# A transformer block on one NeuronCore: order of the row sums, the rotary steps and the head turns, order of the PSUM banks, and fixed places for the first stage's weights

## The chip, the core and the metric

The kernel runs on one core of a Trainium2 chip. The core has five engines that work through their own queues in order and meet at semaphores: TensorE (matmuls and transposes, called PE in the profile, its weight loads PEld), VectorE (DVE), ScalarE (ACT), GpSimd (POOL) and SyncE (SP, which issues most DMAs). Matmul results land in PSUM, eight banks of 128 x 512 float32; everything else lies in SBUF, and large data in HBM.

The metric is the device time of one execution in microseconds. Before the change three runs took 2041.41, 2048.91 and 2049.46 us, median 2048.91.

## The reference, cut to what matters

One encoder layer on 512 tokens of width 2048, everything in float32:

```python
h = rmsnorm(x, g_mix)
qa, ka, va, qb, kb, vb = split(h @ w_in)          # 1024, 256, 256, 1024, 1024, 1024 columns
q, k = axial_rope(rmsnorm(qa, g_q)) * hd**-0.5, axial_rope(rmsnorm(ka, g_k))   # mixer A: 8 heads, 2 kv heads
A = softmax(q @ k.T) @ va
q, k = partial_rope(qb) * hd**-0.5, partial_rope(kb)                            # mixer B: 8 heads
B = softmax(q @ k.T + log_multiplicity_mask) @ vb       # three dilated windows merged by their denominators
x = x + concat(rmsnorm(A, g_out_a), rmsnorm(B, g_out_b)) @ w_out
h2 = rmsnorm(x, g_ffn)
x = x + (silu(h2 @ w_gate) * (h2 @ w_up)) @ w_down
out = rmsnorm(x, g_final)
```

## The kernel before, in words

**Precision.** A float32 product is made of three matmuls. Each operand is split into a high part (ScalarE copies it in a rounded format) and a low part (VectorE subtracts), and `mm3` (line 200) multiplies high by high, high by low, low by high.

**Units.** The weights stream through a list of units in a fixed order, and the order is written out by hand: the main loop (lines 1190 to 1220) goes through the list, and at each unit it emits loads up to 20 or 24 us ahead, splits up to 8 or 10 us ahead (`prepare`, line 1163), then the unit's own matmuls, then what is hooked to that unit, then *side tasks*. Each unit gives a credit (1.0, in the attention 1.42 and later 1.9), and a side task is emitted when the credit covers its cost. So the program's order, and with it the order on each engine's queue, comes from these numbers. A plain unit is 12 matmuls of 512 columns, a block's unit 6.

**The input projection.** The first chunk makes k, v of mixer A (`kvA`, 16 plain units). While it runs, `x_prep` (line 266) transposes x on TensorE and splits it, and `row_squares` (line 317) sums the squares of whole rows on ScalarE, from which `make_r1` gets the row scale that each result is multiplied by when it leaves PSUM. Then come two blocks (`in_block`, line 752): two groups of 512 columns at a time, with seven products of half-size operands in place of eight. Each block's products are named m1 to m7, 8 units each, and accumulate in three pairs of banks, z, y and x. The first block makes vB, the second qA. Four plain chunks follow for qB and kB. All results are written to HBM and read back (`reload`, line 410) when the attention wants them.

**The attention** is made of side tasks beside the four plain chunks and the first half of the output projection. `norm_rope` (line 356) does the norm and the rotary steps of mixer A for one group of 128 tokens in two tasks, `rope_partial` (line 443) those of mixer B. A head takes four slots; in a slot (`task`, line 553) TensorE transposes a block of the probabilities of a head six slots earlier (`pt`), multiplies one of seven slots earlier with v (`pv`), makes one score block (`score`), and three and two slots ahead of a head its q and k are transposed (`tq`, `tk`).

**Memory.** `bank` (line 94) takes PSUM banks from one pool of eight, `Raw.load` (line 215) weight buffers from pools with a count each (`RAWS`), `slot` (line 83) SBUF pieces of 128 x 512; which free piece is taken is left to the framework.

**Behind it** lie the output projection, eleven gate/up blocks and the down projection, in the same form of block.

Of the kernel before, what the change touches and what calls it, by code (L numbers as in the profile page):

```python
# [19 lines left out]
P = 128  # L20
# [30 lines left out]
RAWS = {"raw": 6, "craw": 24, "craw40": 20, "draw6": 20, "draw8": 28}  # L51
W_TILES = {"wi": 12, "wo": 12}
# [5 lines left out]
TURN_LAG = 6  # L58
COLUMN_BLOCKS = 2
# [7 lines left out]
def encoder_block(ctx, tc, x, g_mix, w_in, g_q_a, g_k_a, g_out_a, g_out_b, w_out, g_ffn,  # L67
# [26 lines left out]
    def bank(base):  # L94
        return pp.tile([P, 512], F32, tag="b", bufs=8, name=nm(base))
# [8 lines left out]
    xs = [None] * KD  # L104

    def load_x(k):
        xs[k] = slot(f"x{k}", F32, (P, NT, P))
        nc.sync.dma_start(xs[k], x[0, :, k * P:(k + 1) * P].rearrange("(t p) c -> p t c", p=P))
# [28 lines left out]
    warm_ps = bank("warm")  # L137
# [5 lines left out]
    def load_gain(dst, rows, eng):  # L143
        raw = slot("gain")[:KD, :P]
        lo = 0
        for src, n in rows:
            eng.dma_start(raw[lo:lo + n], src[0].rearrange("(k p) -> k p", p=P))
            lo += n

        def finish():  # L150
            ps = bank("gain")
            nc.tensor.transpose(ps[:, :KD], raw, ident[:KD, :KD])
            nc.scalar.activation(dst, ps[:, :KD], AF.Copy)
        return finish
# [6 lines left out]
    def load_consts():  # L161
        for i, g in enumerate((g_q_a, g_k_a)):
            nc.sync.dma_start(gqk[:, i, :], row_bcast(g, HD))
        for i in range(2):
            ctab.append(slot("ctab", F32, (P, NT, HD)))
            nc.sync.dma_start(ctab[i], c_axial[:, i])
        nc.sync.dma_start(ropeb, c_partial)
        nc.sync.dma_start(mask, c_mask)
# [40 lines left out]
    units = []  # L209

    class Raw:
# [3 lines left out]
        def load(self):  # L215
            if self.t is None:
                self.t = wp.tile([P, self.width], F32, tag=self.tag, bufs=RAWS[self.tag], name=nm("raw"))
                for src, dst in self.pieces(self.t):
                    if self.first:
                        for a in range(src.shape[1]):  # L220
                            nc.sync.dma_start(dst[:, a], src[:, a])
                            load_x(self.first + a)
                    else:
                        nc.sync.dma_start(dst, src)

    class Unit:
# [10 lines left out]
        def split_hi(self):  # L237
            src = self.raw.t[:, self.sub * 512:(self.sub + 1) * 512]
            self.src, self.w = src, (wslot(self.tag), wslot(self.tag))
# [19 lines left out]
    xpair = [None] * (KD // 2)  # L259
# [6 lines left out]
    def x_prep(k):  # L266
        ps = bank("xt")
        for t in range(NT):
            nc.tensor.transpose(ps[:, t * P:(t + 1) * P], xs[k][:, t, :], ident)
        i, half = divmod(k, 2)  # L270
        if half == 0:
            xpair[i] = sp.tile([P, 4 * 512], F32, tag="xpair", bufs=3, name=nm("xpair"))
# [9 lines left out]
        else:  # L282
            nc.scalar.activation(flat, ps, AF.Copy, scale=gain)
            nc.scalar.activation(hi, view, AF.Copy)  # L284
            nc.vector.tensor_tensor(lo, view, f32(hi), op=OP.subtract)
        if half == 0:
# [23 lines left out]
    ss1 = small()  # L310
    rows = {}

    def load_rows(t):
        rows[t] = sp.tile([P, D], F32, tag="rows", bufs=2, name=nm("rows"))
        nc.sync.dma_start(rows[t], x[0, t * P:(t + 1) * P, :])

    def row_squares(t):
        nc.scalar.activation(rows[t], rows[t], AF.Square, accum_out=ss1[:, t:t + 1])

    def col_sums(src):  # L320
        ps = bank("cs")
        for t in range(NT):
            nc.tensor.matmul(ps[:, t:t + 1], src[:, t * P:(t + 1) * P], ones, start=True, stop=True)
        return ps[:, :NT]
# [3 lines left out]
    def make_r1():  # L328
        r1["r"] = rsqrt_mean(ss1, NT, D)
# [3 lines left out]
    tabs = {}  # L333

# [65 lines left out]
    def post_plain(name, ps):  # L400
        for t in range(NT):
            e = slot("ev" + name)
# [3 lines left out]
            else:  # L406
                nc.scalar.activation(e, ps[t], AF.Copy, scale=r1["r"][:, t:t + 1])
            store(name, t, e, nc.scalar)

    def reload(name, dst):  # L410
        assert stored[name] == NT, name
        for t in range(NT):
            dst[t] = slot(name)
            nc.sync.dma_start(dst[t], spill[name][t])

    def split_vA(t):
# [4 lines left out]
        src = kA[t][:, 256:]  # L421
        nc.scalar.activation(h, src, AF.Copy)
        nc.vector.tensor_tensor(l, src, f32(h), op=OP.subtract)

    def transpose_k_a(kv):
        ps = bank("kt")
        for t in range(NT):
            nc.tensor.transpose(ps[:, t * P:(t + 1) * P], kA[t][:, 256 + kv * HD:256 + (kv + 1) * HD], ident)
        kTA[kv] = split(ps, "kT", at=((2, 4 + 2 * kv), (2, 5 + 2 * kv)))

# [30 lines left out]
    class Head:  # L461
# [5 lines left out]
        def tq(self):  # L467
            ps = bank("qt")
# [6 lines left out]
            self.q = split(ps, "qT")  # L475

        def tk(self):
# [3 lines left out]
            ps = bank("kt")  # L481
# [3 lines left out]
            self.k = split(ps, "kT")  # L485

        def score(self, t):
            if t == 0:
                self.negm, self.z, self.rz = small(), small(), small()
            ps = bank("sc")  # L490
# [6 lines left out]
            else:  # L497
# [3 lines left out]
                nc.scalar.activation(p, p, AF.Exp, bias=nmx, scale=-1.0, accum_out=z)  # L501
            nc.vector.reciprocal(rz, z)
# [3 lines left out]
        def pt(self, kb):  # L506
            ps = bank("pt")
            for t in range(NT):
                nc.tensor.transpose(ps[:, t * P:(t + 1) * P], self.p[t][:, kb * P:(kb + 1) * P], ident)
            self.pT = split(ps, "pT")  # L510
            self.pTs = getattr(self, "pTs", {})
            self.pTs[kb] = self.pT

        def pv(self, kb):
            if kb == 0:
                self.o = bank("o")
# [7 lines left out]
        def fin(self):  # L524
# [8 lines left out]
            else:  # L533
                sq = slot("sq")
                nc.scalar.activation(sq, self.o, AF.Square)
                nc.gpsimd.tensor_tensor(acc[self.kind], acc[self.kind], sq, op=OP.add)
            if self.h == 7:
# [7 lines left out]
    def head_tasks(spec):  # L545
        n = len(heads)
        heads.append(Head(*spec))

        def at(slot):
            h, i = divmod(slot, NT)  # L550
            return (heads[h], i) if 0 <= h < len(heads) else (None, i)

        def task(s):
            head, i = at(s - TURN_LAG)
            if head:
                head.pt(i)
            head, i = at(s - TURN_LAG - 1)
            if head:
                head.pv(i)
                if i == NT - 1:  # L560
                    head.fin()
            head, i = at(s)
            if head:
                head.score(i)
            head, i = at(s + 3)
            if head and i == 0:
                head.tq()
            if head and i == 1:
# [706 lines left out]
```

## Time and profile before

| | |
|---|---|
| median of the runs | 2048.91 us |
| profiled execution, its own time | 2048.41 us |
| its span, first to last instruction | 2046.6 us |
| mean granted TensorE clock | 0.990 |
| PE busy | 2002.8 us (98%) |
| DVE busy | 1560.9 us (76%) |
| ACT busy | 1110.0 us (54%) |

A row of the waits view reads: engine and result that waited, what ended the wait, us in total, how often, the longest. A row of a timeline reads: start, duration, engine, line, operation, result and operands, and in brackets the engine's idle time before it with what ended it. A group row gives count, busy us and mean ns, then the idle time before the group. A clock of 0.5 means that TensorE got half of its full clock.

### The profile page before, as it was taken

To read this page: it belongs to the slowest core of one execution; us is meant where nothing else is said; L and a number is where in the kernel's file an instruction comes from. 1 tells how busy PE (TensorE), PEld (TensorE's weight loads), DVE (VectorE), ACT (ScalarE), POOL (GpSimd) and SP (SyncE) were. 2 spreads that over 40 slices of the span, in tenths; PEclk is the share of its full clock that TensorE was granted. 3 is DMA by queue.
4 is the path that set the end of the run, shared out by engine and by line. 5 is a ranking of instruction groups with operands and counts; after the bars stand their busy time and mean duration, and the time that the engine had idled before them with its cause. 6 is when DMAs were issued, how large, how long until landed. Compare 5 with 4: busy or idle time off the path is not lost.

```text
span 2046.6 us, 27457 instructions
## 1 busy us (share of the span) xinstructions
PE 2002.8 (98%) x9019; PEld 1639.0 (80%) x9019; DVE 1560.9 (76%) x2768; ACT 1110.0 (54%) x1952; POOL 126.4 (6%) x155
## 2 busy tenths in 40 slices
PE   9999999999999999999999999999999999999997
PEld 7788877887778888888888888888888888788886
DVE  5778756566764479778778788788788987977876
ACT  7655344455543466545555545545555666656655
POOL 0000101000000000000000000000000021111122
PEclk9999999999899999999999999999999999999999
DMA  8876532235234457458468367477477699778855
GB/s 273 299 249 203 174 103 93 89 117 176 98 97 151 158 180 240 136 197 293 138 217 290 119 239 262 132 254 250 133 252 233 201 282 249 188 172 268 216 115 179
DMA packets 232336, 394.82 MB, mean 193 GB/s; under 512 B 21712, under 2 KB 70656, under 8 KB 231552
## 3 DMA queue, kind: packets, MB, share of 16 engines
q1 hardware_dynamic: 205696, 330.33, 48.0%
q0 software_dynamic: 14800, 32.51, 7.9%
q10 hardware_dynamic: 11696, 30.23, 4.3%
q8 instruction: 70, 1.15, 0.2%
q14 instruction: 74, 0.61, 0.1%
HBM read 329.28 MB, written 63.70 MB: 192 GB/s over the span
## 4 chain that ended last, share of the span: by engine, by line
PE 86%; DVE 6%; issue 3%; ACT 2%; DMA 1%; POOL 1%; ACTq 0%; POOLq 0%; DVEq 0%; SPq 0%
PE zc L202 12%; PE zc L203 12%; PE zc L204 12%; PE yc L203 6%; PE yc L202 6%; PE yc L204 6%; PE xc L202 3%; PE xc L203 3%; PE xc L204 3%; PE pj L204 3%; PE pj L203 3%; PE pj L202 3%; PE pw L202 3%; PE pw L204 3%; PE pw L203 3%
## 5 line engine op out<-in xcount | busy, mean ns | idle before, releaser
L688 ACT ACTIVATE tw<-raw 128x512 fp32r<-128x512 f32 x1036 | 627.1, 628 | 496.1 <-DVE raw L725 321.7
L691 DVE TENSOR_TENSOR tw<-raw,tw 128x512 fp32r<-128x512 f32 x1036 | 693.3, 686 | 186.4 <-ACT tw L688 182.6
L202 PE MATMUL zc<-tw,arena 128*128 128x512 f32 x1184 | 465.6, 393 | 2.5 <-ACT ev L1045 1.7
L203 PE MATMUL zc<-tw,arena 128*128 128x512 f32 x1184 | 463.1, 391 | 4.5 <-DVE tw L691 4.4
L204 PE MATMUL zc<-tw,arena 128*128 128x512 f32 x1184 | 462.7, 391 | 0.0
L725 DVE TENSOR_TENSOR raw<-raw,raw 128x512 f32<-128x512 f32 x592 | 405.1, 684 | 1.4 <-DMA raw<-in_w_gate_up_dram 1.4
L203 PEld LDWEIGHTS zc<-tw,arena 128*128 128x128 f32 x1184 | 223.2, 189 | 52.9 <-DVE tw L691 7.8
L202 PEld LDWEIGHTS zc<-tw,arena 128*128 128x128 f32 x1184 | 223.2, 188 | 49.9 <-ACT ev L1045 2.4
L204 PEld LDWEIGHTS zc<-tw,arena 128*128 128x128 f32 x1184 | 222.9, 188 | 46.7
L202 PE MATMUL yc<-tw,arena 128*128 128x512 f32 x592 | 231.4, 391 | 0.0
L203 PE MATMUL yc<-tw,arena 128*128 128x512 f32 x592 | 230.6, 390 | 0.8 <-DVE tw L691 0.8
L204 PE MATMUL yc<-tw,arena 128*128 128x512 f32 x592 | 230.5, 389 | 0.0
L1046 POOL DMA_DIRECT2D x1d<-ev x76 | 66.4, 971 | 1154.4 <-ACT ev L1045 1142.3
L202 PE MATMUL pj<-w,arena 128*128 128x512 f32 x320 | 129.5, 405 | 3.4 <-ACT arena L284 1.9
L203 PEld LDWEIGHTS yc<-tw,arena 128*128 128x128 f32 x592 | 111.2, 188 | 24.3 <-DVE tw L691 1.7
L204 PEld LDWEIGHTS yc<-tw,arena 128*128 128x128 f32 x592 | 111.1, 188 | 23.2
L202 PEld LDWEIGHTS yc<-tw,arena 128*128 128x128 f32 x592 | 111.1, 188 | 22.8
L203 PE MATMUL pj<-w,arena 128*128 128x512 f32 x320 | 126.2, 395 | 2.2 <-DVE w L245 2.2
L204 PE MATMUL pj<-w,arena 128*128 128x512 f32 x320 | 126.6, 396 | 0.0
L202 PE MATMUL xc<-tw,arena 128*128 128x512 f32 x296 | 115.4, 390 | 0.0
L203 PE MATMUL xc<-tw,arena 128*128 128x512 f32 x296 | 115.3, 389 | 0.1
L204 PE MATMUL xc<-tw,arena 128*128 128x512 f32 x296 | 115.2, 389 | 0.0
(205 smaller groups left out, 2440.1 us busy)
## 6 DMA issues: line engine op xcount, KB each, us to landing
raw<-in_w_gate_up_dram SPq DMA_DIRECT2D x616, 256.0 KB, 5.3
raw<-in_w_in_dram SPq DMA_DIRECT2D x180, 256.0 KB, 4.5
raw<-in_w_down_dram SPq DMA_DIRECT2D x176, 256.0 KB, 7.0
forms<-pair SPq DMA_DIRECT2D x22, 896.0 KB, 5.3
x1d<-ev POOLq DMA_DIRECT2D x76, 256.0 KB, 6.8
fr<-forms ACTq DMA_DIRECT2D x35, 512.0 KB, 4.9
raw<-in_w_out_dram SPq DMA_DIRECT2D x32, 512.0 KB, 4.2
x<-in_x_dram SPq DMA_DIRECT2D x32, 256.0 KB, 4.9
```

The lines of the kernel that those rows point to most:

```text
L202: nc.tensor.matmul(dst, ah, bh, start=start, stop=False, skip_group_check=chained)
L203: nc.tensor.matmul(dst, ah, bl, start=False, stop=False, skip_group_check=chained)
L204: nc.tensor.matmul(dst, al, bh, start=False, stop=stop, skip_group_check=chained)
L688: nc.scalar.activation(self.pair[:, 0], self.src, AF.Copy)
L691: nc.vector.tensor_tensor(self.pair[:, 1], self.src, f32(self.pair[:, 0]), op=OP.subtract)
L725: nc.vector.tensor_tensor(t[dst], t[src[0]], t[src[1]], op=OP.add if form == "m6" else OP.subtract)
L1046: nc.gpsimd.dma_start(x1_dram[2 * cb + j, row], e, accum_op=OP.add)
```

## The change

- **Row sums in halves.** Each row of 2048 is loaded and squared in two halves, eight steps hooked to units 13 to 28 in place of four at units 11 to 14; the row scale is made at unit 29. kvA is therefore written without the scale, and k and v are scaled after their reload (`scale_k`, `split_vA`). The first block's first eviction comes 7 units later.
- **Order of the blocks.** qA first, vB second.
- **Early rotary steps and turns.** Tables and q steps come ahead of v and k. The second group of q steps is spread over slots 6 to 9. B's rotary steps come 8 and 7 slots ahead of their head pair, their reload 11 ahead; q is transposed 4 slots ahead, k 2. The value product comes 8 slots after the score.
- **PSUM banks in order of return.** Eight fixed banks in a queue: `bank()` takes the first, `release` puts a bank back at the end.
- **Fixed places.** Until the second block's end, x, the weights of the first chunk and of both blocks, and kvA's evictions use 20 fixed places of 128 x 512 (24 for a while), taken and returned in the same way; meanwhile only two double buffers of the next chunk's weights may be loaded. Split pairs, rows and results also get fixed tiles.
- **Others.** q, k reload as one transfer each; the constants load later, the mask at slot 20; buffer counts of later stages change (`RAWS`).

```diff
-RAWS = {"raw": 6, "craw": 24, "craw40": 20, "draw6": 20, "draw8": 28}
-W_TILES = {"wi": 12, "wo": 12}
+RAWS = {"raw": 6, "craw": 24, "craw0": 24, "kraw": 9, "craw40": 18, "draw6": 21, "draw8": 28}
+W_TILES = {"wi": 10, "wo": 12}
+VALUE_LAG = 8
-    def bank(base):
-        return pp.tile([P, 512], F32, tag="b", bufs=8, name=nm(base))
+    banks = deque(pp.tile([P, 512], F32, tag=f"b{n}", name=f"b{n}") for n in range(8))
+    def bank():
+        return banks.popleft()
+    def release(*tiles):
+        banks.extend(tiles)
+    stage = wp.tile([P, 20, 512], F32, tag="stage", bufs=1, name="stage")
+    homes = deque(stage[:, n] for n in range(20))
+                self.homed = bool(homes) and self.tag != "raw"
+                self.t = homes.popleft() if self.homed else wp.tile([P, self.width], F32, tag=self.tag,
+                                                                    bufs=RAWS[self.tag], name=nm("raw"))
-    def row_squares(t):
-        nc.scalar.activation(rows[t], rows[t], AF.Square, accum_out=ss1[:, t:t + 1])
+    def load_rows(n):
+        rows[n] = in_turn(rows_turn, 2, [P, D // 2], F32, "rows")
+        t, half = divmod(n, 2)
+        nc.sync.dma_start(rows[n], x[0, t * P:(t + 1) * P, half * (D // 2):(half + 1) * (D // 2)])
+    def row_squares(n):
+        nc.scalar.activation(rows[n], rows[n], AF.Square, accum_out=ss1[:, n:n + 1])
+    for n, at in enumerate((13, 15, 18, 20, 22, 24, 26, 28)):
+        hook(at - 3, lambda n=n: load_rows(n))
+        hook(at, lambda n=n: row_squares(n))
+    hook(29, make_r1)
+    hook(21, more_homes)
-            head, i = at(s - TURN_LAG - 1)
+        head, i = head_at(s - VALUE_LAG)
-            head, i = at(s + 3)
+        for lead in ("tq", "tk"):
+            head, i = head_at(s + {"tq": 4, "tk": 2}[lead])
...
+        todo = light(0.4, table_tasks()) + q_tasks(0)
+        todo += light(0.4, vs + kn)
+        todo += [heads[0].tq] + light(0.6, [lambda kv=kv: transpose_k_a(kv) for kv in range(NKV)])
+        todo += [heads[0].tk]
+        at(3, light(0.1, [lambda: reload("qA1", qA[1])]))
+        at(20, light(0.1, [lambda: nc.sync.dma_start(mask, c_mask)]))
+        for n, f in enumerate(q_tasks(1)):
+            at(6 + n // 2, [f])
+        for j in range(4):
+            s = NT * (NHA + 2 * j)
+            at(s - 11, light(0.1, [lambda j=j: reload(f"qkB{j}", qkB[j])]))
+            for n, f in enumerate(b_ropes(j)):
+                at(s - 8 + n, [f])
...
-    last.after("m5", 0, load_consts)
-    last.after("m5", 3, lambda: reload("kvA", kA))
+    last.after("m3", -2, load_consts)
+    last.after("m3", 0, leave_homes)
+    last.after("m5", 0, fewer_homes)
+    last.after("m3", 1, lambda: reload("qA0", qA[0]))
+    last.after("m3", 2, lambda: reload("kvA", kA))
...
+                    if homing[0] and len(homes) <= (2 if xs[KD - 1] is None else 4 if done["load"] < 24 else 0):
+                        return
+                    if homing[0] and raw.tag == "raw" and sum(r.tag == "raw" for r in live) >= 2:
+                        return
```

295 lines of the change are left out of this document (165 added, 130 removed).

## The prediction

> **What bounds the kernel now.** I began with the page's busy times and clock row, then cut the span into stretches to see where TensorE is not fed.
>
> ```profile
> span 2046.6 us, 27457 instructions
> PE 2002.8 (98%) x9019; PEld 1639.0 (80%) x9019; DVE 1560.9 (76%) x2768; ACT 1110.0 (54%) x1952; POOL 126.4 (6%) x155
> PEclk9999999999899999999999999999999999999999
> ```
>
> TensorE is busy 2002.8 of 2046.6 us. The change neither adds nor removes a matmul of 512 columns, so it can only win what TensorE loses to waits and to a reduced clock. The stretches show where that is; the columns are length, busy time (instructions) of PE, PEld, DVE, ACT and POOL, granted clock, DMA share, GB/s.
>
> ```profile
> 50.00:100.00 50.00, 45.21 (x187) 34.79 (x186) 38.28 (x70) 32.23 (x53) 2.75 (x4) 0.97 0.88 311
> 150.00:200.00 50.00, 50.00 (x222) 41.42 (x221) 41.33 (x68) 25.77 (x43) 1.64 (x3) 1.00 0.58 194
> 250.00:300.00 50.00, 44.86 (x199) 36.34 (x199) 31.00 (x74) 18.07 (x40) 2.23 (x2) 0.93 0.36 106
> 300.00:350.00 50.00, 45.62 (x207) 35.01 (x206) 34.04 (x94) 19.68 (x42) 4.45 (x4) 1.00 0.27 89
> 450.00:500.00 50.00, 47.95 (x236) 38.45 (x235) 32.69 (x79) 28.27 (x60) 3.58 (x3) 1.00 0.45 144
> 500.00:550.00 50.00, 43.94 (x207) 34.80 (x205) 38.13 (x95) 26.02 (x53) 2.60 (x2) 0.93 0.49 162
> 550.00:600.00 50.00, 45.41 (x212) 36.18 (x212) 35.67 (x86) 25.15 (x53) 3.88 (x3) 0.93 0.24 75
> 600.00:650.00 50.00, 49.69 (x214) 39.70 (x215) 18.95 (x30) 21.61 (x39) 3.99 (x3) 0.94 0.47 157
> ```
>
> The stretch 150:200 is the undisturbed one: 222 matmuls in 50 us, 0.225 us each. Idle time in the other seven is 4.8 + 5.1 + 4.4 + 2.1 + 6.1 + 4.6 + 0.3 = 27.4 us. A clock of 0.93 over 50 us is 3.5 us of lost work, so the clock adds 1.5 + 3.5 + 3.5 + 3.5 + 3.0 = 15 us. Together 42 us lie in the projection and the attention, which this change rewrites; the gate/up and down stages behind them it touches only in buffer counts.
>
> The waits say who is late.
>
> ```profile
> PE qt L474 <- DVE qkB L453: 5.7, 8, 1.7
> PE qt L474 <- DVE qA L383: 5.1, 2, 4.2
> PE pt L509 <- DVE pTl L194: 3.1, 4, 1.4
> PE pj L203 <- DVE w L245: 2.2, 3, 1.4
> PE kt L484 <- DVE qTl L194: 2.1, 3, 0.7
> PE pj L202 <- ACT evqkB L405: 1.5, 4, 0.6
> PE o L203 <- DVE pTl L194: 1.5, 2, 1.3
> ```
>
> No engine is full here (DVE 31 to 38 of 50 us): TensorE waits because in-order queues reach a piece of work late, or because a PSUM bank is taken that was read a moment ago (pt, kt and pj<-evqkB: a transpose or matmul waits for the *previous* tile's last read).
>
> **Term A, row sums in halves (50 to 100 us).** ScalarE there:
>
> ```profile
> 43.99 1.90 ACT L318 ACTIVATE rows<-rows 128x2048 f32<-128x2048 f32 x1
> 45.80 0.18 ACT L318 ACTIVATION_READ_ACCUMULATOR rows<-rows 128x1 f32 x1
> 46.59 0.63 ACT L284 ACTIVATE arena<-xpair 128x512 fp32r<-128x512 f32 x1
> 56.55 1.92 ACT L318 ACTIVATE rows<-rows 128x2048 f32<-128x2048 f32 x1 [0.46 <-DMA rows<-in_x_dram]
> 64.22 0.69 ACT L407 ACTIVATE evkvA<-pj,smalls 128x512 f32<-128x512 f32 x1 [1.82 <-POOL smalls L184]
> 49.66 0.33 SPq L315 DMA_DIRECT2D rows<-in_x_dram  x1
> ```
>
> Four squares of 1.90 + 0.18 us fall into 14 us, then the kvA evictions wait 1.8 us for the row scale. After the change eight halves are spread over units 13 to 28 of the stream, and kvA is stored unscaled, so nothing at unit 15 waits. A half, interpolated between the 0.63 us row and the 1.90 us row, is 1.04 + 0.18 = 1.2 us; eight are 9.8 us against 8.3, which is 1.5 us more ScalarE work, hidden because it is spread over 16 units. Added too are four scalings of 256 columns for k (0.5 us each) after the reload. Against it: a half's buffer comes back only four column units (4 x 6 x 0.225 = 5.4 us) before its next square, and 1.2 us of that is the square. The last whole row was issued at 49.7 and used at 56.6, 6.9 us, so a half may land up to 2.7 us late, in two chains of buffers; if the 8 us by which splits run ahead did not hide that, it costs 4 us. Between -4 and the whole 6.3 us I take 4, nearer the gain since the split lead lies between.
>
> **Term B, the turn from the blocks to attention (250 to 300 us).** DVE had a hole at the turn, and ScalarE shows why.
>
> ```profile
> 223.94 0.42 DVE L423 TENSOR_TENSOR arena<-kvA,arena 128x256 fp32r<-128x256 f32 x1 [5.12 <-ACT arena L422]
> 220.63 0.69 ACT L764 ACTIVATE evqA<-zc,smalls 128x512 f32<-128x512 f32 x1 [7.48 <-PE zc L204]
> 218.82 2.81 SPq L414 DMA_DIRECT2D qA<-qA  x4
> 242.60 0.28 DVE L366 CUSTOM_DVE_ANT_0 ra<-qA 128x128 f32<-128x128 f32 x1
> 246.42 0.69 DVE L383 TENSOR_TENSOR qA<-qA,smalls 128x512 f32<-128x512 f32 x1
> 260.11 0.69 DVE L383 TENSOR_TENSOR qA<-qA,smalls 128x512 f32<-128x512 f32 x1
> ```
>
> DVE stands 5.1 us for a V split that sits on ScalarE behind the block's last eviction, is then full from 223.9 to 260.8, and the first query transpose, which needs the last rotary step, waits for it. The change puts the tables and the query steps first, which need no ScalarE; the block order makes qA old enough to be read. The hole can go. But what is late next is the load: qA's reload is now one transfer of 1 MB, behind some three weight pairs of 512 KB on SP's queue, since these were held to two while the fixed stage lived; and the two key transposes move to the end of the list, with only one query transpose between them and the last k step. DVE's work from 223.9 to 260.8 is 36.9 us, some 4 of them around the key transposes, so 33; begun at 218.8 it ends at 252. TensorE comes to that point at 260.8 - 5.1 = 255.7. The lead is 4 us, and a longer hole while qA lands brings the wait back. Whole gain: 5.1 + 3.5 clock = 8.6. If 2.6 MB at 194 GB/s (the stretch 150:200) keep qA until some 13 us after 218.8, the wait is 4 us longer than now: -4. I take 4, between the ends, nearer the gain since the weights were prefetched in part.
>
> **Term C, second group of query steps (300 to 350 us).** One token's query steps take DVE 4.5 us (242.60 to 247.1). Eight tasks of cost 0.8 stood in a row; at 1.42 per unit of 12 matmuls (2.7 us) two of them give TensorE 3.1 us. So DVE fell behind by over 1 us per token, and its weight splits with it (pj<-w). Now a score slot of cost 1.5 stands between each pair: 2.9 us of projection and six matmuls more, while DVE has the following to do for a slot.
>
> ```profile
> L194 DVE TENSOR_TENSOR pTl<-pt,pTh 128x512 fp32r<-128x512 f32 x64 | 44.0, 688 | 48.5 <-ACT pTh L193 47.9 <-issue 0.5
> L503 DVE TENSOR_SCALAR p<-p,smalls 128x512 f32<-128x512 f32 x64 | 34.0, 531 | 2.2
> L495 DVE TENSOR_REDUCE smalls<-sc 128x1 f32<-128x512 f32 x32 | 22.0, 689 | 7.7 <-PE sc L204 6.3
> L502 DVE RECIPROCAL smalls<-smalls 128x1 f32<-128x1 f32 x64 | 10.5, 164 | 59.2 <-ACT p L496 30.5 <-ACT p L501 28.7
> ```
>
> That is 2.1 us and a weight split, 2.8, against 4.3 or more on TensorE. The backlog shrinks in the slot, and I take 3.4 of the 4.4 us (bounds 0 and 4.4).
>
> **Term D, the heads (450 to 620 us).** These are the first query transposes of a B head pair after its rotary steps:
>
> ```profile
> 509.62 0.33 PE L474 MATMUL qt<-fixed,qkB 128*128 128x128 f32 x1 [1.66 <-DVE qkB L453]
> 510.54 0.37 PE L474 MATMUL qt<-fixed,qkB 128*128 128x128 f32 x1 [0.59 <-DVE qkB L453]
> 511.46 0.47 PE L474 MATMUL qt<-fixed,qkB 128*128 128x128 f32 x1 [0.56 <-DVE qkB L453]
> 512.39 0.48 PE L474 MATMUL qt<-fixed,qkB 128*128 128x128 f32 x1 [0.45 <-DVE qkB L453]
> 514.25 1.12 PE L509 MATMUL pt<-fixed,p 128*128 128x128 f32 x4 [1.39 <-DVE pTl L194]
> ```
>
> The steps stood one task ahead of the transposes; now they stand three slots ahead, over 10 us, with the same instructions. Of the 5.7 us of qt<-qkB I expect all. Banks handed out in order of return mean that a taker gets the one longest idle: kt<-qTl 2.1 and pt<-pTl 3.1 go (half of them lie in 450 to 620). The value product is two slots behind its transpose instead of one: o<-pTl, 1.5 us, mostly goes. I take 9.5 of the 13.1 us idle here. Of the three reduced clocks (10 us) I take two, 7: each stands in a stretch with such waits. Bounds: 3 (banks only) to 23.
>
> Here a rule speaks against me. The Trainium skill, TensorE: Matmul & The Clock Gate, Why this matters for your kernels, asks only for "No PE-idle gaps >~3µs between matmul bursts" to keep the clock. By it the three late reductions, where no wait is over 1.7 us, would have another cause and stay, and the time would be 7 us higher, 2024. The trace disagrees with it: 0.93 stands beside waits of 1.7, 0.6, 0.6, 0.5 and 1.4 us in a row.
>
> **Term E, the rest.** A wait's end costs a little that busy time hides (single transposes above of 0.33 to 0.48 us): some 30 waits less by 0.1 us, 3 us. The buffer counts of the last gate/up block (20 to 18) and the first down blocks (20 to 21) bind where a load is late; I take 0, bounds -3 and +1 (a wait like those of 0.6 to 1.9 us above, once or twice). First-chunk splits in eight pairs instead of six, two copies of 4 columns and the mask's later load lie beside other work: 0, or -1 where uncovered.
>
> Sum: 4 + 4 + 3.4 + 16.5 + 3 = 31 us. The profiled execution took 2048.4 us, 1.8 around its span and 0.5 below the median of the runs shown, 2048.9. So 2017; terms moving together within half their bounds make 2009 to 2026.
>
> **The rivals.**
> *Only the heads gain* (0.15). A and B come to nothing, because ScalarE waits for halves and the turn waits for qA's load. For: 50 to 100 us moves 311 GB/s at a DMA share of 0.88. Against: the split lead. Then C, D and 2 of E, 22 us, less the 4 that one of them may cost: 2030.
> *All of it goes* (0.12): 42 + 4, 2002. For: no engine is full; against: B's thin lead.
> *The order only changes who is last* (0.12). The chain score, DVE, ScalarE, DVE, transpose, ScalarE, DVE limits the heads, and TensorE waits at pt instead of qt. For: ScalarE ends 47.9 us of DVE's gaps. Against: those gaps cost TensorE nothing for most heads. Then D gives 3, the others half: about 9, so 2040, within 0.5%.
> *Room in SBUF decides* (0.11), and it is slower. The stage of 20 places, q and k reloaded as whole 1 MB tiles, and one more pair of transposed probabilities per head all lie in one memory. If a head's slots must wait for the value product two slots behind, every score slot waits. SP already waits for such room:
>
> ```profile
> SPq L436 <- DVE pTl L194: 23.3, 3, 15.7
> ```
>
> It decides once ScalarE's p or pT waits for a release instead of for data; one 0.6 us wait (as pj<-evqkB) in each of 64 + 9 slots is 44 us, so 2048 - 31 + 44 = 2061. Against: the stage ends before attention.
>
> **How the numbers follow.** Forecast 0.50. About 0.5% (10 us) is what a measurement of this kernel can tell from none, that is 2038.7 to 2059.2. Faster is 0.50 + 0.15 + 0.12 = 0.77, same 0.12, slower 0.11. The range 2003 to 2045 leaves out slower and a little of the full gain.
>
> **What would show it.** A: no square of 2048 columns, no zc<-tw wait before 80 us, clock 1.00 there. B: no 5 us hole in DVE at the turn, and qt<-qA gone; wrong if kt (its keys) waits instead. C: pj<-w under 1 us. D: qt<-qkB, kt<-qTl, pt<-pTl gone, clock 1.00 from 500 to 620. Wrong altogether if ScalarE's or DVE's waits inside the slots are ended by older slots' reads.

## The result, and the profile after

The changed kernel takes 2024.82 us (2023.18 to 2026.50), the kernel before 2048.16 us over all its runs beside it: a ratio of 0.9893, with a 95% interval of 0.9869 to 0.9916. That is a gain of 23.3 us, where 31 were predicted. The profiled execution took 2025.08 us. These are the page's span and busy times of the changed kernel:

```profile
span 2023.3 us, 27380 instructions
PE 1989.5 (98%) x9019; PEld 1632.9 (81%) x9019; DVE 1558.8 (77%) x2771; ACT 1112.5 (55%) x1964; POOL 125.9 (6%) x155
```

The same 9019 matmuls and transposes are busy for 13.3 us less, and the span outside them is shorter by 10.0 us (33.8 in place of 43.8). So over half of the gain is in *shorter* busy time, and nearly all of that is the granted clock: its mean rose from 0.990 of the 2046.6 us to 0.996 of the 2023.3, some 12 us of lost clock less. Only the rest of the gain is idle time that a view of waits would list.

The stretches of the changed kernel, with the columns of the prediction (length, busy time of PE, PEld, DVE, ACT, POOL, granted clock, DMA share, GB/s):

```profile
50.00:100.00 50.00, 47.14 (x196) 36.57 (x195) 36.95 (x69) 33.45 (x61) 2.74 (x4) 0.97 0.71 242
100.00:150.00 50.00, 47.47 (x210) 38.99 (x209) 38.91 (x64) 26.40 (x44) 2.16 (x4) 1.00 0.69 247
250.00:300.00 50.00, 50.00 (x238) 41.43 (x237) 34.05 (x84) 22.07 (x49) 2.92 (x3) 1.00 0.38 125
300.00:350.00 50.00, 48.09 (x226) 39.28 (x225) 32.53 (x78) 24.20 (x52) 3.51 (x3) 0.97 0.27 85
450.00:500.00 50.00, 45.58 (x215) 36.10 (x214) 33.48 (x83) 27.94 (x59) 2.35 (x2) 0.97 0.51 165
500.00:550.00 50.00, 46.89 (x234) 37.09 (x232) 37.62 (x91) 27.09 (x56) 3.86 (x3) 1.00 0.41 130
550.00:600.00 50.00, 49.58 (x248) 40.73 (x249) 32.44 (x70) 27.07 (x54) 6.58 (x5) 1.00 0.39 126
600.00:650.00 50.00, 50.00 (x222) 41.39 (x221) 21.34 (x34) 16.14 (x27) 0.00 (x0) 1.00 0.41 138
```

The stretch 100 to 150, which was nearly full, has become worse. The kernel before had there:

```profile
100.00:150.00 50.00, 49.90 (x221) 40.94 (x220) 38.07 (x63) 26.32 (x43) 2.17 (x4) 1.00 0.68 232
```

If idle time and lost clock (50 us less the granted share) are added up for each term's stretches as the prediction did, before and after, the account is the table below. It is rough by about a microsecond for each term, since the later stages now begin 8 us earlier and more, and by the clock: a 0.97 or a 0.93 over 50 us is one stretch at half clock, of some 3.4 or 6.8 us, and such stretches come and go between runs with the same waits (see the late rotary steps and the last section).

| term, stretch | lost before | lost after | gain | predicted |
|---|---|---|---|---|
| A, 50 to 150 | 4.8 + 0.1 + 1.5 = 6.4 | 2.9 + 2.5 + 1.5 = 6.9 | -0.5 | 4 |
| B, 250 to 300 | 5.1 + 3.5 = 8.6 | 0 | 8.6 | 4 |
| C, 300 to 350 | 4.4 | 1.9 + 1.5 = 3.4 | 1.0 | 3.4 |
| D, 450 to 650 | 13.1 + 10 = 23.1 | 7.9 + 1.5 = 9.4 | 13.7 | 16.5 |
| E, the rest | | | 0.5 (23.3 less the others) | 3 |

TensorE's waits up to 640 us in the changed kernel (result, releaser: us in total, times, longest). All PSUM tiles are called b now; L576 is the transpose of the probabilities, L538 that of q, L230 and L231 are the first two of the three matmuls.

```profile
PE b L576 <- DVE pTl L222: 5.0, 4, 2.4
PE b L230 <- DVE pTl L222: 3.4, 4, 1.9
PE b L230 <- ACT ends L840: 2.5, 1, 2.5
PE b L231 <- DVE tw L758: 1.5, 5, 0.5
PE b L230 <- ACT tw L755: 1.3, 1, 1.3
```

The two largest waits of before, for qkB (5.7) and for qA (5.1), have gone, and those for w and for qTl before a key transpose with them. The value product no longer waits for its low part (o <- pTl, 1.5 before). Two have grown or come new: the waits for a bank that the split of transposed probabilities still reads (L576 and L230 <- pTl, 8.4 in place of the 3.1 of pt <- pTl) and one wait of 2.5 us for the first block's eviction (ends). The rows of L230 are not value products that lack their low part: L230 multiplies the high parts, and three of its four waits (at 333, 519 and 538 us) are scores, which take no pT at all. The longest of them:

```profile
333.22 0.50 PE L230 MATMUL b<-arena,qTh 128*128 128x512 f32 x1 [1.91 <-DVE pTl L222]
```

### The profile page after: what moved, and what is told of

Its sections match the earlier page's. It is cut to its first block, busy times and chain, and to the rows that moved or that the text cites. A ratio compares the mean times of both kernels' runs of the same rounds, so it can differ in the third digit from the quotient of the medians.

```text
span 2023.3 us, 27380 instructions
## 1 busy us (share of the span) xinstructions
PE 1989.5 (98%) x9019; PEld 1632.9 (81%) x9019; DVE 1558.8 (77%) x2771; ACT 1112.5 (55%) x1964; POOL 125.9 (6%) x155
## 5 line engine op out<-in xcount | busy, mean ns | idle before, releaser
L230 PE MATMUL b<-tw,arena 128*128 128x512 f32 x2136 | 838.5, 393 | 7.2 <-ACT ends L840 2.5
L231 PE MATMUL b<-tw,arena 128*128 128x512 f32 x2136 | 834.0, 390 | 5.4 <-DVE tw L758 5.1
L232 PE MATMUL b<-tw,arena 128*128 128x512 f32 x2136 | 832.8, 390 | 0.0
L755 ACT ACTIVATE tw<-raw 128x512 fp32r<-128x512 f32 x924 | 559.3, 628 | 441.2 <-DVE raw L792 286.6
L758 DVE TENSOR_TENSOR tw<-raw,tw 128x512 fp32r<-128x512 f32 x924 | 619.3, 687 | 173.1 <-ACT tw L755 170.1
L231 PEld LDWEIGHTS b<-tw,arena 128*128 128x128 f32 x2136 | 401.6, 188 | 93.3 <-DVE tw L758 12.3
L230 PEld LDWEIGHTS b<-tw,arena 128*128 128x128 f32 x2136 | 401.4, 188 | 90.7 <-ACT tw L755 3.3
L232 PEld LDWEIGHTS b<-tw,arena 128*128 128x128 f32 x2136 | 401.4, 188 | 83.9
L230 PE MATMUL b<-w,arena 128*128 128x512 f32 x368 | 146.7, 399 | 0.0
L232 PE MATMUL b<-w,arena 128*128 128x512 f32 x368 | 144.3, 392 | 0.0
L231 PE MATMUL b<-w,arena 128*128 128x512 f32 x368 | 144.1, 392 | 0.0
L232 PEld LDWEIGHTS b<-w,arena 128*128 128x128 f32 x368 | 69.5, 189 | 15.1
L231 PEld LDWEIGHTS b<-w,arena 128*128 128x128 f32 x368 | 69.6, 189 | 13.9
L230 PEld LDWEIGHTS b<-w,arena 128*128 128x128 f32 x368 | 69.5, 189 | 13.7
L758 DVE TENSOR_TENSOR tw<-stage,tw 128x512 fp32r<-128x512 f32 x93 | 62.2, 687 | 23.5 <-ACT tw L755 23.4
L755 ACT ACTIVATE tw<-stage 128x512 fp32r<-128x512 f32 x93 | 56.5, 627 | 41.8 <-DVE stage L792 29.5
L287 DVE TENSOR_TENSOR w<-raw,w 128x512 fp32r<-128x512 f32 x96 | 64.7, 684 | 5.7 <-ACT ends L840 3.0
L1126 ACT ACTIVATE ev<-b,smalls 128x512 f32<-128x512 f32 x76 | 49.7, 683 | 29.2 <-PE b L232 28.0
```

Of the source, the lines that this page charges most:

```text
L230: nc.tensor.matmul(dst, ah, bh, start=start, stop=False, skip_group_check=chained)
L231: nc.tensor.matmul(dst, ah, bl, start=False, stop=False, skip_group_check=chained)
L232: nc.tensor.matmul(dst, al, bh, start=False, stop=stop, skip_group_check=chained)
L287: nc.vector.tensor_tensor(self.w[1], self.src, f32(self.w[0]), op=OP.subtract)
L755: nc.scalar.activation(self.pair[:, 0], self.src, AF.Copy)
L758: nc.vector.tensor_tensor(self.pair[:, 1], self.src, f32(self.pair[:, 0]), op=OP.subtract)
```

## The experiments

Each difference is of the experiment's median against 2024.82, or against the kernel named; each ratio is against the kernel before, on the same chip.

**The order of the PSUM banks.** The eight queued banks become one pool again:

```diff
-    banks = deque(pp.tile([P, 512], F32, tag=f"b{n}", name=f"b{n}") for n in range(8))
     def bank():
-        return banks.popleft()
+        return pp.tile([P, 512], F32, tag="b", bufs=8, name=nm("b"))
     def release(*tiles):
-        banks.extend(tiles)
+        pass
```

> The changed kernel with the PSUM banks taken again from one pool of eight, whichever the framework picks; all else as changed (2024.8 us). Theory: a bank that was read a moment ago is taken again, the waits kt<-qTl and pt<-pTl of before come back (about 5 us) with some 3 us of reduced clock: 2031 to 2034. Rival: the value product's two slots and the early turns already keep banks apart, so nothing moves: 2023 to 2027.

Measured: 2024.58 us, ratio 0.9887 (0.9872 to 0.9901). Its waits:

```profile
PE b L574 <- DVE pTl L220: 5.0, 4, 2.4
PE b L228 <- DVE pTl L220: 3.4, 4, 1.8
```

They are the same as with the queue, to 0.1 us. The bank order is worth nothing here, and kt <- qTl stays away without it.

**Late rotary steps.** B's rotary steps and the transposes of q go back to where they stood, everything else stays changed:

```diff
-            head, i = head_at(s + {"tq": 4, "tk": 2}[lead])
+            head, i = head_at(s + {"tq": 3, "tk": 2}[lead])
-            at(s - 11, light(0.1, [lambda j=j: reload(f"qkB{j}", qkB[j])]))
+            at(s - 5 if j else s - 9, light(0.1, [lambda j=j: reload(f"qkB{j}", qkB[j])]))
-                at(s - 8 + n, [f])
+                at(s - 4 if j else s - 5, [f])
```

> The changed kernel with mixer B's rotary steps and their reload put back to one task ahead of the query transposes, and the query transposed 3 slots ahead as before; all else as changed. Theory of the prediction: the waits of the query transposes for the rotary steps return, 5 to 6 us, and two reduced clocks with them, 6 to 7 us: 2034 to 2038. Rival (the order only changes who is last): under 4 us, 2025 to 2029.

Measured: 2031.78 us, 7.0 more, between what the theory and the rival expected; ratio 0.9924 (0.9904 to 0.9943). Its wait:

```profile
PE b L538 <- DVE qkB L517: 6.1, 7, 1.9
```

and one of its stretches:

```profile
500.00:550.00 50.00, 45.66 (x199) 35.79 (x199) 36.31 (x88) 24.83 (x52) 2.60 (x2) 0.88 0.36 119
```

The wait returns as large as before (6.1 for 5.7), and the clock falls to 0.88 with it: two groups of such waits, at 495 and at 540 us, each have some 6.8 us at half clock behind them. TensorE's rows at the first:

```profile
495.42 0.33 PE L538 MATMUL b<-fixed,qkB 128*128 128x128 f32 x1 [1.39 <-DVE qkB L517]
496.34 0.33 PE L538 MATMUL b<-fixed,qkB 128*128 128x128 f32 x1 [0.59 <-DVE qkB L517]
498.52 0.48 PE L538 MATMUL b<-fixed,qkB 128*128 128x128 f32 x1 [1.85 <-DVE qkB L517]
499.44 0.48 PE L538 MATMUL b<-fixed,qkB 128*128 128x128 f32 x1 [0.45 <-DVE qkB L517]
500.14 0.63 PE L231 MATMUL b<-arena,arena 128*128 128x512 f32 x1
500.57 0.63 PE L232 MATMUL b<-arena,arena 128*128 128x512 f32 x1
...
505.91 0.40 PE L232 MATMUL b<-pTh,vl 128*128 128x512 f32 x1
```

After four waits, none over 1.85 us, a matmul starts every 0.43 us instead of every 0.23 and takes 0.63 instead of 0.40, for about 5 us. The Trainium skill (TensorE: Matmul & The Clock Gate, Why this matters for your kernels) allows idle gaps up to about 3 us; these rows disagree with it. That it is the group of waits that does it is not shown: a single wait of 2.42 us has half clock behind it too, for 3.4 us in the changed kernel and for 6.8 in the one with the pool of banks, and at the same place, after 2.48 us, there is none with the three fixed pairs below. In that order (length, busy times, clock, DMA):

```profile
494.00:498.00 4.00, 3.65 (x11) 3.08 (x12) 3.08 (x8) 2.30 (x5) 0.00 (x0) 0.57 0.33 126
494.00:502.00 8.00, 6.76 (x20) 5.52 (x21) 5.72 (x14) 4.25 (x9) 0.00 (x0) 0.57 0.51 167
488.00:492.00 4.00, 4.00 (x20) 3.39 (x21) 3.08 (x8) 2.30 (x5) 0.00 (x0) 1.00 0.24 66
```

A clock of 0.57 over 4 us is 1.7 us lost, which is 3.4 us at half. So a difference of 1.7 or 3.4 us between two kernels can be clock alone.

**The keys first.** At the turn the keys' transposes and the v and k steps go ahead of the q steps, and their reload first, as before:

```diff
-        todo = light(0.4, table_tasks()) + q_tasks(0)
+        todo = light(0.4, table_tasks())
         todo += light(0.4, vs + kn)
-        todo += [heads[0].tq] + light(0.6, [lambda kv=kv: transpose_k_a(kv) for kv in range(NKV)])
-        todo += [heads[0].tk]
+        todo += light(0.6, [lambda kv=kv: transpose_k_a(kv) for kv in range(NKV)]) + q_tasks(0)
+        todo += [heads[0].tq] + [heads[0].tk]
```

> The changed kernel with the old order at the turn: tables, then v and k steps and the key transposes, then the query steps and the first query transpose; kvA reloaded ahead of qA. Theory: the hole of 5 us in VectorE's queue comes back, the first query transpose waits as before, with a reduced clock: 7 to 8 us more, 2031 to 2033. Rival: the order of the blocks and the earlier loads removed the hole, not the order of the steps: 2024 to 2027.

Measured: 2033.41 us, 8.6 more; ratio 0.9926 (0.9910 to 0.9942). Its wait at the turn:

```profile
PE b L538 <- DVE qA L440: 5.2, 2, 4.2
```

That is the old wait (5.1, 2, 4.2) once more. The median rises by 8.6 us, as much as the turn had lost before; that the two agree so well is luck, as the profiled execution, the fastest of the four, is 5.3 us above the change's and loses 5.2 us idle and a clock of 0.97 in 250 to 300. To put back the order of the steps and of the two reloads is enough to lose term B; the new order of the blocks does not keep it. In the changed kernel VectorE goes through the turn like this:

```profile
219.78 0.69 DVE L287 TENSOR_TENSOR w<-raw,w 128x512 fp32r<-128x512 f32 x1 [2.98 <-ACT ends L840]
220.39 0.28 DVE L423 CUSTOM_DVE_ANT_0 ra<-qA 128x128 f32<-128x128 f32 x1
```

A hole of 3.0 us is left, behind the block's last evictions on ScalarE, in front of a weight split. The q steps then start at once: qA had landed, and neither qt nor kt waits.

**The lag of the value product.** Seven slots in place of eight:

```diff
-VALUE_LAG = 8
+VALUE_LAG = 7
```

> The changed kernel with the value product one slot behind the transpose again (7 slots behind the score instead of 8). Theory: the value product waits for the low part again in the heads, 1.5 to 3 us and perhaps one reduced clock: 2027 to 2031. Rival: the split is done in time either way, and the slot more only keeps tiles longer: 2023 to 2026.

Measured: 2033.76 us, 8.9 more; ratio 0.9927 (0.9910 to 0.9943), more than expected. The wait behind it in this kernel:

```profile
PE b L231 <- DVE pTl L222: 6.2, 7, 1.8
```

In the kernel before, with the same lag of seven, o <- pTl stood at 1.5 us. Of the 6.2, 1.8 is one value product of mixer A at 337 us, behind the late split that makes a score wait 1.9 us in the changed kernel. The rest lies in mixer B's heads; 2.5 us of it, at 512, 523 and 544 us, has no like in the kernel before, where TensorE, held up at qt, came late to the value product. The waits do not make up the 8.9 us: the profiled execution, the slowest of the four and 11.2 us above the change's, is idle for 4.5 us more and busy for 6.8 more, of which its clock explains about 2.

**Three parts undone together.** Late rotary steps, keys first and lag seven in one kernel, by the three diffs above:

> The changed kernel with three orders put back at once: mixer B's rotary steps late, v and k ahead of q at the turn, the value product one slot behind its transpose. Row halves, bank order, fixed places, block order and the spread of the second query group stay. Theory: these three orders are the whole gain (each alone cost 7.0, 8.6 and 8.9 us when undone): 2045 to 2051, the time before. Rival: they overlap, or the parts that stay are worth something by themselves: 2033 to 2042.

Measured: 2041.00 us, 16.2 more; ratio 0.9965 (0.9952 to 0.9978). Singly the three cost 7.0 + 8.6 + 8.9 = 24.5 us; together 16.2. Two of its waits show the overlap:

```profile
PE b L538 <- DVE qkB L517: 6.5, 8, 1.9
PE b L231 <- DVE pTl L222: 2.2, 4, 1.4
```

With late rotary steps the short lag costs 2.2 us of waits and with early ones 6.2; of the 4.0 us between them some 2 are the waits at 512 to 544 us named above, and 1.8 the one at 337. What the change gains without the three (halves, places, the spread second group, block order, bank order, buffer counts) is 2048.58 - 2041.00 = 7.6 us.

**The loads of the half rows.** Six of the eight loads of half rows are left out; the squares run on what lies in the buffers:

```diff
-        nc.sync.dma_start(rows[n], x[0, t * P:(t + 1) * P, half * (D // 2):(half + 1) * (D // 2)])
+        if n < 2:
+            nc.sync.dma_start(rows[n], x[0, t * P:(t + 1) * P, half * (D // 2):(half + 1) * (D // 2)])
```

> The changed kernel with only the first two of the eight half-row loads; the other six squares run over the same two buffers again, so the row scale and all that follows is not the reference's. Theory: in the changed kernel ScalarE waits 6.7 us for late half rows, and the TensorE waits at 83, 92 and 111 us with the reduced clock there follow from it; without the loads they go: 2018 to 2020. Rival: ScalarE's and VectorE's own work at the start of the first block is too much, the waits stay: 2023 to 2026.

Measured: 2016.36 us, 8.4 less, more than expected; ratio 0.9843 (0.9826 to 0.9861). Its stretch:

```profile
50.00:100.00 50.00, 49.16 (x216) 39.70 (x215) 43.15 (x79) 37.64 (x68) 2.74 (x4) 1.00 0.55 179
```

and its wait for the first eviction:

```profile
PE b L230 <- ACT ends L841: 0.9, 1, 0.9
```

The idle time of the stretch falls from 2.9 to 0.8 us and its clock stands at 1.00, which it also does with late rotary steps, where the halves are as late; the eviction's wait falls from 2.5 to 0.9. So late halves do reach TensorE: from 50 to 150 us its idle time falls by 3.7 of the 8.4 us, and the stretch of half clock there goes. In the changed kernel, SP's queue and then ScalarE show how:

```profile
70.16 0.43 SPq L360 DMA_DIRECT2D rows<-in_x_dram  x1
70.64 1.85 SPq L259 DMA_DIRECT2D more<-in_w_in_dram  x4
72.59 0.89 SPq L259 DMA_DIRECT2D stage<-in_w_in_dram  x2
73.57 0.48 SPq L360 DMA_DIRECT2D rows<-in_x_dram  x1
```

```profile
74.58 1.06 ACT L363 ACTIVATE rows<-rows 128x1024 f32<-128x1024 f32 x1 [1.89 <-DMA rows<-in_x_dram]
81.15 1.06 ACT L363 ACTIVATE rows<-rows 128x1024 f32<-128x1024 f32 x1 [4.38 <-DMA rows<-in_x_dram]
```

A half issued at 70.16 is used at 74.58, 4.4 us later; the next, issued at 73.57 behind six weight loads, at 81.15, 7.6 us later. ScalarE stands 4.4 us before that square, with the weight splits behind it; TensorE waits 1.35 us at 82.9 (the 1.3 of tw L755 above) and half a microsecond at 92.

**The halves earlier.** Same work, hooked 4 to 5 units sooner:

```diff
-    for n, at in enumerate((13, 15, 18, 20, 22, 24, 26, 28)):
+    for n, at in enumerate((9, 11, 13, 15, 17, 19, 21, 23)):
```

> The changed kernel with the eight half rows loaded and squared at units 9, 11, ... 23 in place of 13 to 28, so that their loads come ahead of the time when the weights fill the DMA queues; all else as changed. Theory: ScalarE no longer waits for rows, 4 to 6 us less: 2019 to 2021. Rival: the loads collide with the first chunk's weights and x instead, or ScalarE is late in the first chunk: 2024 to 2030.

Measured: 2021.48 us, 3.3 less; ratio 0.9871 (0.9854 to 0.9889), an interval that overlaps with the change's own. Its stretch:

```profile
50.00:100.00 50.00, 48.92 (x216) 39.24 (x215) 40.85 (x75) 35.02 (x62) 2.74 (x4) 1.00 0.75 249
```

Most of the idle time of 50 to 100 us goes, 1.1 us in place of 2.9, with the same bytes and the same squares, and ScalarE waits 2.1 us for halves in place of 6.7. The 2.5 us wait for the first block's eviction stays as it was, at 107.6 us now.

**The first block in the common order of products.** On top of the early halves:

```diff
-                   chain=("m1", "m2", "m7", "m6", "m5", "m4", "m3") if first else CHAIN)
+                   chain=CHAIN)
```

> The kernel with early half rows (2021.5 us), and the first block's products in the order of all other blocks (m1, m7, m6, m2, m5, m4, m3), so that m5 does not follow m6 in the same bank. Theory: the 2.5 us wait of TensorE for the eviction of m6 at 105 us goes, with its reduced clock (1.7 us): 2017 to 2019. Rival: m7 needs two weights per unit and comes 8 units earlier, so weights or sums of x are late: 2022 to 2030.

Measured: 2026.05 us, 4.6 more than the early halves alone; ratio 0.9889 (0.9874 to 0.9903). The special order is no fault: without it the wait for the eviction (L230 <- ends) grows to 4.2 us.

**Three fixed pairs for the transposed probabilities.** With the early halves, the split of pT gets three pairs of tiles of its own instead of pieces from the common pool:

```diff
-            self.pTs[kb] = split(ps, "pT")
+            hi, lo = in_turn(pts, 3, [P, 512], F32R, "pt"), in_turn(ptl, 3, [P, 512], F32R, "ptl")
+            nc.scalar.activation(hi, ps, AF.Copy)
+            nc.vector.tensor_tensor(lo, ps, f32(hi), op=OP.subtract)
+            self.pTs[kb] = (hi, lo)
```

> The kernel with early half rows (2021.5 us), and three fixed pairs for the transposed probabilities instead of slots that the framework picks. In the changed kernel VectorE waited 6.2 us once, at 332 us, for the store of a result that lay in the slot it was given, ScalarE twice for some 2 us. Theory: these waits and the 1.9 us wait of TensorE behind the first go, 1 to 4 us less: 2018 to 2020. Rival: with less room the other slots wait instead: 2021 to 2026.

Measured: 2017.14 us, 4.3 less than the early halves alone; ratio 0.9841 (0.9824 to 0.9857), and the two intervals touch. What it cures is this row of the changed kernel, where a split waits not for its data but for a piece that a store to HBM still reads:

```profile
332.48 0.69 DVE L222 TENSOR_TENSOR pTl<-b,pTh 128x512 fp32r<-128x512 f32 x1 [6.19 <-DMA qkB<-evqkB]
```

TensorE waits 1.9 us for it, and the clock of 300 to 350 is 0.97. In the kernel with the early halves the split waits 5.6 us and the stretch is idle for 1.2 us, at clock 1.00. With the fixed pairs it is full:

```profile
300.00:350.00 50.00, 50.00 (x245) 41.13 (x244) 33.99 (x76) 24.83 (x54) 3.51 (x3) 1.00 0.33 104
```

So 1.2 of the 4.3 us are this wait. In the profiled executions another 1.7 are the half clock that does not follow the wait at 488 us here (above), and for that no run gives a reason.

**Without the scaling of p.** VectorE's reciprocal and scaling of the probabilities are left out:

```diff
-            nc.vector.reciprocal(rz, z)
-            nc.vector.tensor_scalar(p, p, rz, None, op0=OP.mult)
```

> The changed kernel without the division of the probabilities by their sum (reciprocal and product left out in all 64 score slots, so the attention's output is not the reference's); 0.65 us less VectorE work per slot. Theory: the waits that are left in the heads (transposes of probabilities waiting 5.0 us for the last low part) come from VectorE's and ScalarE's turn within a slot, so they shrink to under 2.5 us and the time by 3 to 8 us: 2017 to 2022. Rival: the waits hang on the number of free banks or on ScalarE alone and stay: 2023 to 2026.

Measured: 2020.36 us, 4.5 less; ratio 0.9864 (0.9849 to 0.9879), an interval that overlaps with the change's own.

```profile
PE b L574 <- DVE pTl L222: 4.0, 3, 2.5
PE b L230 <- DVE pTl L222: 1.4, 3, 0.6
```

Some 44 us of VectorE work less take 3 us from these waits, and the longest, 2.5 us, stays. So the amount of VectorE's work does not make that wait. In the changed kernel, ScalarE, VectorE and TensorE before that wait:

```profile
489.87 0.60 ACT L599 ACTIVATE acc<-b 128x512 f32<-128x512 f32 x1 [1.84 <-PE b L231]
```

```profile
491.20 0.17 DVE L569 RECIPROCAL smalls<-smalls 128x1 f32<-128x1 f32 x1 [1.55 <-ACT p L567]
492.33 0.75 DVE L225 SCALAR_TENSOR_TENSOR arena<-oback,fixed,arena 128x512 fp32r<-128x512 f32 x1 [0.45 <-ACT arena L224]
493.60 0.69 DVE L222 TENSOR_TENSOR pTl<-b,pTh 128x512 fp32r<-128x512 f32 x1
```

```profile
488.66 0.60 PE L576 MATMUL b<-fixed,p 128*128 128x128 f32 x4
494.35 1.01 PE L576 MATMUL b<-fixed,p 128*128 128x128 f32 x4 [2.42 <-DVE pTl L222]
```

The transpose at 494.35 waits for the low split of the one at 488.66. In this stretch the half of the output projection holds four banks and a head's result one, so three are left, and in between they went to a score (490.52) and to the transposes of q (491.32): by this count the third next taker gets the same bank, in any order of handing out. That split comes 4.9 us after its transpose because ScalarE stood 1.84 us for TensorE's value product (acc), and VectorE 1.55 and 0.45 us for ScalarE, with two other pieces of work ahead of the split in its queue. It is a round trip through three in-order queues, and the matmuls behind the wait then run at half pace (clock 0.57 from 494 to 498, above).

**One slot more between transpose and value product,** with the early halves:

```diff
-VALUE_LAG = 8
+VALUE_LAG = 9
```

> The kernel with early half rows (2021.5 us) and the value product three slots behind its transpose (9 slots behind the score). Theory: the step from one slot to two took 9 us away; what is left of the value product's wait, 2.6 us, goes with a third: 2017 to 2020. Rival: a tile more is kept, the framework's slots become short and waits on stores and older reads rise: 2022 to 2030.

Measured: 2015.63 us, 5.9 less than the early halves alone, more than expected; ratio 0.9841 (0.9824 to 0.9857). The wait of the transposes:

```profile
PE b L576 <- DVE pTl L222: 3.8, 3, 2.6
```

It falls from 5.0 to 3.8, with one wait of 2.6 us left, and that of L230 from 2.6 to 2.0. These are waits for banks; the value product's own wait, which the expectation took the 2.6 for, was gone with a lag of eight. Both together fall by 1.8 us of the 5.9; where the rest lies (short waits within busy time and clock, as far as the profile can show) isn't resolved, and the two intervals touch.

**The first block's eviction earlier.** Early halves, three fixed pairs, the row scale made at unit 24 and the first eviction 3 units later in place of 7:

```diff
-    hook(29, make_r1)
+    hook(24, make_r1)
-        rows_of("m1", 0, 0, begin, 7 if first else 0)
+        rows_of("m1", 0, 0, begin, 3 if first else 0)
```

> The kernel with early half rows and three fixed pairs (2017.1 us), with the row scale made at unit 24 and the first block's first eviction 3 units after m1 instead of 7. Theory: ScalarE and VectorE win lead for m6's eviction, whose 2.5 us wait at 105 us shrinks: 2014 to 2016. Rival: the lead in m7 and m6 is set by VectorE's two steps per unit (1.2 us of the unit's 1.365), the wait stays: 2016 to 2018.

Measured: 2014.49 us (2013.70 to 2017.78), ratio 0.9838 (0.9824 to 0.9853). The wait for the eviction (L230 <- ends) is 2.2 in place of 2.5, and the median 2.6 us below that with the fixed pairs alone, within both kernels' spread. Making the scale and the first eviction earlier is not what that eviction needed; its cause stays open. This is the fastest version measured, 10.3 us below the change, and level with the one of lag nine.

## Why the prediction was right and wrong

The direction, the place and the kind of the gain were right, and the time is 7.8 us above the forecast. Step by step:

**A, row sums in halves: failed.** The step that failed is that the splits' lead would hide a half that lands late. The prediction had its price (a half up to 2.7 us late, 4 us lost) and took the good side. The latest half came 4.4 us late. The price was about right for the stalls (50 to 100 us loses 4.4 us in the changed kernel and 1.1 with the earlier halves; the medians lie 3.3 apart too, though their intervals overlap); it was the sign that failed. Taking the loads away gives 8.4 us, but that takes six loads and 1.6 us of the eviction's wait with it. "No zc<-tw wait before 80 us" held only to the letter: the waits moved to 82.9 and 92. A half took 7.6 us to land behind weight loads on SP's queue, where the sum had 6.9 and only 4.2 us between buffer and square. The second half of the failure was not in the sum at all: the 2.5 us wait for the first block's eviction is new. That the eviction comes later is not its reason, as it stays at 2.2 us with the first eviction four units sooner; without the loads of the halves it is 0.9, and more the runs do not show. Rival 1's first half, ScalarE waiting for halves, is what happened; its second half, the turn waiting for qA's load, did not.

**B, the turn: right, and larger.** All 8.6 us came. The feared load landed in time, since qA is reloaded first. Taking 4, between the ends, left 4.6 us out. VectorE's hole shrank from 5.1 to 3.0 us instead of going, and no longer counts, since the q steps have lead enough.

**C, the second group: the mechanism right, part of the gain given back.** pj <- w is gone. In its place stands one split that waits 6.2 us for a store's piece of SBUF, 1.9 us on TensorE and a stretch of half clock. With the fixed pairs 300 to 350 us is full: this is the mechanism of the last rival (room in SBUF), at one place instead of in every slot. No run undid the spread of the second group alone, so that it is what removed pj <- w is argued from the rows and not shown.

**D, the heads: right on the steps and the lag, wrong on the banks.** The early rotary steps do what was said, 7.0 us for 5.7 of waits with their clock. "kt<-qTl 2.1 and pt<-pTl 3.1 go" because of the bank order is the step that failed: the pool gives the same waits to 0.1 us, and pt <- pTl grew to 5.0, with 3.4 us more of the same kind, mostly at scores. kt <- qTl did go, with or without the bank order; the earlier transposes of q are the likely reason, since with late ones (the run with late rotary steps) a 0.7 us wait of that kind is back. The lag did end o <- pTl. Sized at 1.5 us, it is worth 8.9 once the rotary steps no longer hold TensorE up, of which the waits explain a part. The third rival, that the order only changes who is last, names that effect; the lag, it seems, is what kept it from deciding. Of the reduced clocks two were expected to go; the three of 500 to 650 went, and one of 0.97 came at 494.

**E, the rest: not borne out.** The balance outside A to D is 0.5 us in place of 3. The step that failed is that each wait's end costs busy time: with some 12 us of lost clock taken out of the 13.3, about 1 us of busy time is left for it. The single transposes of 0.47 and 0.48 us on which the term rested stand in a stretch of reduced clock (0.93). The stages behind the attention even lost a little, at the way from the gate/up blocks to the down projection. That stretch in the changed kernel, then in the kernel before:

```profile
1700.00:1800.00 100.00, 96.01 (x414) 77.32 (x415) 81.25 (x124) 61.93 (x101) 15.72 (x18) 1.00 0.74 192
```

```profile
1700.00:1800.00 100.00, 97.24 (x423) 78.61 (x422) 79.40 (x120) 62.65 (x103) 17.45 (x20) 1.00 0.85 228
```

It loses 4.0 us in place of 2.8, and 1350 to 1700 us, where the kernel before was full, loses 1.0 more. That makes 2.2 us, twice the bound of +1 for the buffer counts; no run undid them alone.

So 31 fell to 23.3 by A (-4.5), C (-2.4), D (-2.8) and E (-2.5), and B gave 4.6 back. That these sum to the difference is by the table's construction. That late halves and the store's piece cost TensorE time, and that the bank order gives nothing, is shown by the runs; the share of each to a microsecond is not, the less so as one stretch of half clock is 1.7 us. No run undid the whole-row sums, the places, the spread second group, the order of the blocks or the buffer counts alone; their part is known only within the 7.6 us that the other three leave.

## What to carry to other kernels

When a wait of the busiest engine is removed, look at what that wait had been covering: here a lag whose waits came to 1.5 us behind a late operand has 6.2 us of waits, and costs 8.9 us, once that operand is early, so undo parts together as well as singly. A split load must be placed by its own queue: a smaller piece behind the same weight loads lands no earlier, and issuing it four to five units sooner took most of the stall away with the same bytes. Cycling PSUM banks gave nothing here, where five of eight are held by long accumulations; count how many rotate. Look up which matmul a wait belongs to before naming its cause, and read differences of 1.7 or 3.4 us against the clock of both runs.

## What the runs showed of the hardware that was not expected

The reduced clock of these traces comes in stretches of about 3.4 or 6.8 us at half pace, and the length of the wait ahead of it does not say which. Four waits of 1.4, 0.6, 1.9 and 0.5 us within 4.5 us had 6.8 us behind them. Single waits of 2.42, 2.42 and 2.48 us at one place of the program had 3.4, 6.8 and none in three kernels. The wait for the first block's eviction, 2.53 us both times, had none in the changed kernel (clock 1.00 from 110 to 114 us) and 3.4 with the early halves (0.57 from 108 to 112). The wait of 4.2 us for qA had a clock of 0.93 over its 50 us in the kernel before and 0.97 with the keys first. What else decides, no run here shows.

A half row landed 4.4 us after its issue with one weight load issued since the half before it, 7.6 us with six, and the next one, behind those six and two more, after 7.5 us (76.33 to 83.80), in a stretch that moved less than before (242 GB/s at a DMA share of 0.71, against 311 at 0.88). So the landing went with the loads issued ahead of it rather than with the traffic of the stretch, though no run changed those loads alone.
